# A two-layer hybrid decoder trunk on one core: GpSimd left with the triangular solves alone, and new costs in the list scheduler

## The chip, the core and the metric

The kernel runs on one core of a Trainium2 chip. The core has five engines that each work through a queue of their own in order: TensorE (PE: matrix products, with weight loads listed as PEld), VectorE (DVE), ScalarE (ACT), GpSimd (POOL) and SyncE (SP), which here issues the DMAs. The metric is device time in microseconds from the first to the last instruction with what lies around them; the median of three runs counts. Differences of about 0.2% can be told from none.

## What is computed

Two layers of width D = 1024 over T = 512 tokens, each with a token mixer, cross-attention into 256 memory tokens, and a SwiGLU block; then a last norm. The core of the reference:

```python
for l in range(DEPTH):
    h = rms_norm(x, norm_mix[l])
    p_a, p_b, p_c, p_d = jnp.split(h @ w_in[l], splits, axis=-1)
    y = jnp.concatenate([
        rglru_group(p_a, ...),       # conv, gates, linear scan h_t = a_t h_(t-1) + u_t
        retention_group(p_b, ...),   # chunked decay attention, 4 heads of 64, head norm, silu gate
        rwkv7_group(p_c, ...),       # state_t = state_(t-1)(w_t - kk_t (kk_t a_t)^T) + v_t k_t^T; head norm, gate
        ssd_group(p_d, ...),         # conv, chunked decay attention, gate, group norm
    ], axis=-1)
    x = x + y @ w_out[l]
    x = x + memory_cross_attention(rms_norm(x, ...), rms_norm(mem, ...), mem_wq[l], mem_wk[l], mem_wv[l], mem_wo[l])
    x = x + swiglu(rms_norm(x, ...), ffn_w_in[l], ffn_w_out[l])
return rms_norm(x, norm_final)
```

All is float32, and the result is held to float32 accuracy.

## The kernel before

**Products.** Activations are kept transposed, channels on the 128 partitions and 512 tokens along the row, so that x is eight tiles of 128x512. PE's fast format (fp32r) keeps fewer bits than float32; each operand is therefore split into a rounded part and a rest. `split` (L594) does so for activations and `weights` (L608) for weight blocks of 128x1024: a DMA brings the raw block (tile kind u), ACT copies it into the rounded part (v), and a subtraction gives the rest (w), on DVE or, where the argument `eng` says so, on POOL. `mm3` (L623) then makes three matmuls: rounded by rounded, rounded by rest, rest by rounded. `project` (L633) is a whole projection of 128 channels: one weight block and 24 matmuls of 128x512 into an accumulator in PSUM (kind a).

**The stages of a layer.** `mix` (L1317) normalizes x with `normed` (L712: a product with the norm's factor on DVE for each of eight tiles, the "hats", and its split), makes the memory's keys (`kv.k`, products of 256 columns that cover the start), the mixed inputs of RWKV (`rwkv_mixed`, `rwkv_pair`), and then four groups that run side by side. For RWKV the recurrence is solved in chunks: `rwkv_solve` (L1163) works out 31 dependent steps of two small POOL operations each on a tile n and a tile s and sends the result through DRAM buffers (fd) back into tiles that were set to zero first; `rwkv_whole` and `rwkv_scan` (L1233) go on with 64x64 products over eight chunks. `ssd`, `retention` and `lru` with their `_gate` functions give the other groups; `head_norm` (L971) normalizes heads. At the mixer's end stand the gates, whose projections go through `late` (L1352). `cross` and `ffn` follow. In this text a layer's start is the making of the hats, the solve's end is where the solved tiles come back to PE, and the mixer's end is the gates and head norms ahead of the output projection.

**What sets the order.** Nothing is issued as it is written. Every call is recorded as an `Op` with the tiles it reads and writes (`Sched.record`, L291); `Sched.cost` (L365) gives it a planned duration and latency; `Sched.order` (L402) is a list scheduler: over all engines it takes the operation that can start earliest by plan, with ties broken by the key in L445 (class 0 before 1 before 2, then the longest remaining path). Class 2 are the dense projections, which fill PE between the links of the chains. `place` finds a free buffer of the kind: there are 71 tiles s, three each of u, v and w, three accumulators a, five PSUM banks b. The engines then get their instructions in that order, and each engine's queue is in order: an instruction that waits holds up all behind it. Since all calls are issued at one place, L515 (`op.fn(...)` in `issue`), every row of the profile has that line; operations are told apart by tile names and shapes.

Of the kernel before, what the change touches and what calls it, by code (L numbers as in the profile page):

```python
# [18 lines left out]
T = 512  # L19
# [213 lines left out]
class Op:  # L233
    __slots__ = ("n", "eng", "fn", "args", "kw", "dur", "lat", "preds", "succ", "left", "ready", "end", "rank", "cls",
                 "roots", "first", "chain", "bytes", "start", "table")


def _free(x):
    return int(np.prod(x.shape[1:]))

# [15 lines left out]
class Sched:  # L256
# [108 lines left out]
    def cost(self, op, fn, out, ins):  # L365

        n = _free(out)
        op.bytes = 0
        op.table = None
        op.lat = 170.0  # L370
        in_psum = any(isinstance(x, Ref) and x.root.kind in "ab" for x in ins)
        if "dma" in fn:
            op.bytes = n * out.shape[0] * 4
            op.dur = 1040.0 if op.eng == "POOL" else 470.0
            op.lat = 1700.0 + op.bytes / 350.0
        elif op.eng == "PE":
            op.lat = 200.0
            if fn == "transpose":
                op.dur = 112.0
            else:  # L380
                m, w = _free(ins[0]), _free(ins[1])
                op.dur = (max(2 * m, w) / 2.4 if ins[0].ap.dtype == F32R else max(m, w) * 1.667) + 4
        elif op.eng == "ACT":
            op.dur = 0.83 * n + (60 if in_psum else 95) + sum(c for k, c in (("scale", 140), ("bias", 50)) if isinstance(op.kw.get(k), Ref))
            f = op.args[2] if fn == "activation" else None
            op.table = {AF.Sqrt: 1, AF.Tanh: 0, AF.Exp: 0}.get(f)
        elif op.eng == "DVE":
            n = max([n] + [_free(x.ap) for x in ins])
            rate = 1.04
            if fn == "reciprocal":  # L390
                rate = 6.3
            elif fn in ("tensor_scalar", "tensor_copy", "memset") and not in_psum:
                rate = 0.52
            op.dur = rate * n + 68
            if n > 64 and any(isinstance(x, Ref) and _free(x.ap) == 1 for x in ins):
                op.dur += 60
        else:
            rate = {"tensor_tensor": 2.3, "tensor_copy": 3.5, "memset": 0.83}.get(fn, 1.2)
            op.dur = rate * n + (60 if fn != "tensor_tensor" else 110)


    def order(self, reserve):  # L402
# [26 lines left out]
        side = wire = 0.0  # L429
        table = None  # L430
# [54 lines left out]
        return out  # L485

# [31 lines left out]
class Trunk:  # L518
# [75 lines left out]
    def split(self, src, scale=None, n=T, eng=None):  # L594

        hi, lo = self.S(F32R), self.S(F32R)
        self.split_to(hi[:, :n], lo[:, :n], src, scale, eng)
        return hi, lo

    def split_to(self, hi, lo, src, scale=None, eng=None):  # L600
        if scale is None:
            self.A.copy(hi, src)
            (eng or self.V).tensor_tensor(lo, src, hi.bitcast(F32), op=ALU.subtract)
# [4 lines left out]
    def weights(self, src, kt, cols, eng=None, parts=1, between=lambda: None):  # L608
# [3 lines left out]
        with self.s.mode(0, "w"):  # L612
            n = kt // parts
            for i in range(parts):
# [5 lines left out]
                (eng or self.V).tensor_tensor(lo[:, ks], r[:, ks], h[:, ks].bitcast(F32), op=ALU.subtract)  # L620
# [12 lines left out]
    def project(self, w_dram, c0, xs, eng=None):  # L633
# [3 lines left out]
        for u0 in range(0, nk, 8):  # L637
            kt = min(8, nk - u0)
            h, lo = self.weights(w_dram[u0 * P:(u0 + kt) * P, c0:c0 + P], kt, P, eng)
# [72 lines left out]
    def normed(self, xs, gain):  # L712
# [101 lines left out]
    def ssd(self, l, proj, dtcum):  # L814
# [11 lines left out]
        for j in range(4):  # L826
# [50 lines left out]
            for g in range(2):  # L877
                V.scalar_tensor_tensor(yy[g][:, tk], xs[g][:, tk], self.d["dh", l][:, g:g + 1], yb[:, g * P:(g + 1) * P],
                                       op0=ALU.mult, op1=ALU.add)
                if j:  # L880
                    G.tensor_tensor(yy[g][:, tk], yy[g][:, tk], yi[:, g], op=ALU.add)
# [34 lines left out]
    def lru(self, l, proj):  # L916
# [6 lines left out]
        for i in range(2):  # L923
# [23 lines left out]
            G.tensor_tensor(ti, ti, rc, op=ALU.mult)  # L947
            res.append((a, ti, t))
        for y, (a, ti, t) in zip(yy, res):

            self.s.link(last, A.activation(t, t, AF.Sqrt), True)
            G.tensor_tensor(ti, ti, t, op=ALU.mult)
# [3 lines left out]
    def lru_gate(self, l, proj, yy):  # L956
        V, A = self.V, self.A
        res = []
        for i in range(2):
# [7 lines left out]
            self.G.tensor_tensor(yy[i], q, yy[i], op=ALU.mult)  # L967
# [3 lines left out]
    def head_norm(self, y, eps, eng):  # L971
# [8 lines left out]
        eng.tensor_tensor(y3, y3, over(m), op=ALU.subtract)  # L980
# [4 lines left out]
        eng.tensor_tensor(y3, y3, over(self.rsqrt(m[:, n:], n)), op=ALU.mult)  # L985

    def retention(self, l, proj, vals):
# [62 lines left out]
        for t in yt:  # L1050
            self.head_norm(t, 1e-5, G)
# [9 lines left out]
    def ret_gate(self, l, proj, yy):  # L1061
        res = []
        for i in range(2):
            g = self.two_silu(proj(COL_B + 768 + i * P))
            self.G.tensor_tensor(yy[i], yy[i], g, op=ALU.mult)
# [97 lines left out]
    def rwkv_solve(self, l, nd):  # L1163


        A, G = self.A, self.G
# [24 lines left out]
        for k, f in enumerate((rt, rf)):  # L1191
# [41 lines left out]
    def rwkv_scan(self, l, pairs, RT):  # L1233


        V, A, E, G = self.V, self.A, self.E, self.G
# [6 lines left out]
        for hf in range(2):  # L1243
            for e in range(2):
                t = self.S()
                self.s.link(self.solved, G.memset(t, 0.0), False)
# [46 lines left out]
        for i in range(2):  # L1293
            y = yt[i]
            self.head_norm(y, HD * 1e-5, V)
# [21 lines left out]
    def mix(self, l, xs, kv):  # L1317
# [32 lines left out]
        late = lambda c0: self.project(w, c0, hat, self.G)  # L1350
        with part("rwkv_gate"):
            rc = self.rwkv_gate(l, lora, late, yc)  # L1352
        with part("ssd"):
            rd = self.ssd_gate(l, late, yd)
        with part("ret"):
            rb = self.ret_gate(l, late, yb)
        with part("lru"):
            ra = self.lru_gate(l, late, ya)
# [3 lines left out]
    def mem_stats(self, xs):  # L1362

        V, A, E, G = self.V, self.A, self.E, self.G
        s = None
        for m in xs:
            sq = self.S()

            self.s.link(self.s.anchor, G.tensor_tensor(sq, m, m, op=ALU.mult), False)
            if s is None:  # L1370
                s = sq
            else:
                G.tensor_tensor(s, s, sq, op=ALU.add)
# [197 lines left out]
class MemKV:  # L1571


    def weights(self, d, **k):
        tr = self.tr
        early = self.l == 0
        return tr.weights(tr.a["mem_wk"][self.l][:, d * P:(d + 1) * P], KD, P, tr.V if early and d in (0, 1, 2, 3, 4) else tr.G,
                          2 if early and d < 3 else 1, **k)
# [51 lines left out]
    def v(self, dh):  # L1630
# [3 lines left out]
        for u in range(4):  # L1634
            h, wl = tr.weights(tr.a["mem_wv"][self.l][u * 256:(u + 1) * 256, dh * T:(dh + 1) * T], 2, T, None if dh else tr.G)
# [31 lines left out]
```

## Time and profile before

| | before |
|---|---|
| median of three runs | 1724.83 us (1724.72 to 1726.2) |
| profiled execution | 1725.3 us |
| its span, first to last instruction | 1723.5 us |
| mean granted TensorE clock | 0.985 |
| PE busy | 1662.0 us (96%) in 8344 matmuls |
| DVE busy | 1017.1 us (59%) |
| ACT busy | 631.1 us (37%) |
| POOL busy | 220.1 us (13%) in 240 instructions |

A row of a timeline gives start and duration in us, engine, line, operation, the tile written, the tiles read, their shapes and a count of like instructions that follow each other; a bracket gives how long the engine had been idle before, and what ended that. Tile kinds: s 128x512 in SBUF, t a narrow tile, a and b PSUM accumulators and banks, u, v, w a weight block raw, rounded and rest, prm and cst parameters and constants, n the solve's tile, fd its DRAM buffer. A matmul's row has the size of its stationary operand (128*128) before the shape that it writes; its duration overlaps the next one's, so the distance of two starts is what one costs. The granted clock is given as a share of 2.4 GHz.

### The profile page before, as it was taken

To read this page: it belongs to the slowest core of one execution; us is meant where nothing else is said; L and a number is where in the kernel's file an instruction comes from. 1 tells how busy PE (TensorE), PEld (TensorE's weight loads), DVE (VectorE), ACT (ScalarE), POOL (GpSimd) and SP (SyncE) were. 2 spreads that over 40 slices of the span, in tenths; PEclk is the share of its full clock that TensorE was granted. 3 is DMA by queue.
4 is the path that set the end of the run, shared out by engine and by line. 5 is a ranking of instruction groups with operands and counts; after the bars stand their busy time and mean duration, and the time that the engine had idled before them with its cause. 6 is when DMAs were issued, how large, how long until landed. Compare 5 with 4: busy or idle time off the path is not lost.

```text
span 1723.5 us, 21453 instructions
## 1 busy us (share of the span) xinstructions
PE 1662.0 (96%) x8344; PEld 1354.3 (79%) x8344; DVE 1017.1 (59%) x1700; ACT 631.1 (37%) x962; POOL 220.1 (13%) x240
## 2 busy tenths in 40 slices
PE   7898998999999999999989989999999999999997
PEld 6686776888788888888887867778887888888886
DVE  7766668675665554432467656876665645554323
ACT  6434234444442332222345333454443422332221
POOL 2316025300000000000050421351000000000001
PEclk9998999999999999999999999999999999999999
DMA  7434121441333333333453341116322333233331
GB/s 232 124 100 109 39 55 52 150 141 55 92 98 97 89 96 98 95 98 106 142 163 87 99 92 52 47 61 190 92 79 88 91 98 98 87 97 92 95 95 62
DMA packets 312901, 169.49 MB, mean 98 GB/s; under 512 B 35936, under 2 KB 300384, under 8 KB 312672
## 3 DMA queue, kind: packets, MB, share of 16 engines
q1 hardware_dynamic: 312800, 168.12, 34.1%
q8 instruction: 66, 1.08, 0.3%
q14 instruction: 35, 0.29, 0.1%
HBM read 156.56 MB, written 9.44 MB: 96 GB/s over the span
## 4 chain that ended last, share of the span: by engine, by line
PE 82%; DVE 6%; POOL 3%; ACT 1%; issue 1%; DMA 1%; SPq 1%; DVEq 0%; POOLq 0%; ACTq 0%
PE a L515 73%; PE b L515 10%; DVE s L515 4%; DVE t L515 2%; POOL s L515 2%; POOL n L515 2%; ACT s L515 1%; SPq L515 1%; ACT v L515 0%; DVE w L515 0%; DMA s<-fd 0%; DMA n<-nd 0%; DMA s<-in_lora_dram 0%; DMA nd<-s 0%; DVEq L1663 0%
## 5 line engine op out<-in xcount | busy, mean ns | idle before, releaser
L515 PE MATMUL a<-s,v 128*128 128x512 f32 (+1 forms) x4012 | 1242.5, 389 | 14.5 <-ACT s L515 8.9
L515 PEld LDWEIGHTS a<-s,v 128*128 128x128 f32 x4012 | 748.9, 190 | 174.5 <-ACT s L515 9.7
L515 PE MATMUL a<-s,w 128*128 128x512 f32 (+1 forms) x2006 | 781.9, 390 | 2.8 <-POOL w L515 1.7
L515 ACT CAST v<-u 128x1024 fp32r<-128x1024 f32 (+3 forms) x275 | 282.2, 1027 | 681.1 <-PE a L515 380.7
L515 PEld LDWEIGHTS a<-s,w 128*128 128x128 f32 x2006 | 381.5, 190 | 83.7 <-POOL w L515 1.9
L515 DVE TENSOR_TENSOR w<-u,v 128x1024 fp32r<-128x1024 f32 (+3 forms) x242 | 293.1, 1212 | 154.3 <-ACT v L515 150.9
L515 DVE TENSOR_TENSOR s<-a,s 128x512 f32<-128x512 f32 (+1 forms) x132 | 90.7, 691 | 260.9 <-PE a L515 242.2
L515 ACT ACTIVATE s<-s 128x512 f32<-128x512 f32 (+3 forms) x229 | 142.1, 628 | 123.9 <-DVE s L515 110.1
L515 PE MATMUL b<-s,s 128*64 128x64 f32 (+8 forms) x1268 | 151.3, 273 | 17.3 <-DVE s L515 6.1
L515 POOL TENSOR_TENSOR w<-u,v 128x1024 fp32r<-128x1024 f32 x33 | 82.6, 2507 | 640.7 <-ACT v L515 609.1
L515 PEld LDWEIGHTS b<-s,s 128*128 128x128 f32 (+3 forms) x1268 | 122.1, 167 | 53.0 <-issue 16.0
L515 DVE TENSOR_TENSOR s<-s,s 128x512 f32<-128x512 f32 (+3 forms) x184 | 133.8, 733 | 27.4 <-ACT s L515 21.4
L515 POOL TENSOR_TENSOR s<-s,s 128x512 f32<-128x512 f32 (+3 forms) x45 | 54.7, 1229 | 688.3 <-ACT s L515 561.4
L515 DVE SCALAR_TENSOR_TENSOR s<-s,s 128x512 f32<-128x512 f32 (+2 forms) x164 | 115.9, 711 | 23.4 <-ACT s L515 22.8
L515 DVE TENSOR_TENSOR s<-s,a 128x512 f32<-128x512 f32 (+1 forms) x49 | 33.2, 677 | 100.9 <-PE a L515 100.9
L515 DVE SCALAR_TENSOR_TENSOR s<-s,prm,s 128x512 fp32r<-128x512 f32 (+3 forms) x78 | 63.1, 833 | 8.8 <-ACT s L515 8.5
L515 PE MATMUL a<-v,s 128*128 128x260 f32 (+1 forms) x256 | 66.7, 343 | 0.0
L515 ACT COPY s<-b 64x256 f32<-64x256 f32 (+3 forms) x92 | 30.5, 353 | 98.2 <-PE b L515 96.5
L515 PE MATMUL b<-cst,s 128*128 128x128 f32 (+2 forms) x312 | 52.4, 281 | 6.8 <-POOL s L515 3.2
L515 PEld LDWEIGHTS b<-cst,s 128*128 128x128 f32 x312 | 41.7, 172 | 15.4 <-POOL s L515 4.1
L515 ACT CAST s<-s 128x512 fp32r<-128x512 f32 x48 | 29.5, 620 | 62.1 <-DVE s L515 57.0
L515 DVE SCALAR_TENSOR_TENSOR s<-a,prm,s 128x511 f32<-128x511 f32 (+2 forms) x64 | 47.6, 744 | 2.0 <-ACT s L515 1.2
(94 smaller groups left out, 788.5 us busy)
## 6 DMA issues: line engine op xcount, KB each, us to landing
u<-in_ffn_w_in_dram SPq DMA_DIRECT2D x88, 512.0 KB, 3.7
u<-in_w_in_dram SPq DMA_DIRECT2D x52, 512.0 KB, 3.8
u<-in_ffn_w_out_dram SPq DMA_DIRECT2D x32, 512.0 KB, 3.7
u<-in_mem_wv_dram SPq DMA_DIRECT2D x16, 512.0 KB, 3.6
u<-in_w_out_dram SPq DMA_DIRECT2D x16, 512.0 KB, 3.9
u<-in_mem_wq_dram SPq DMA_DIRECT2D x16, 512.0 KB, 3.8
u<-in_mem_wo_dram SPq DMA_DIRECT2D x16, 512.0 KB, 3.7
u<-in_mem_wk_dram SPq DMA_DIRECT2D x13, 512.0 KB, 3.8
```

Of the source, the lines that this page charges most:

```text
L515: op.fn(*[real(x) for x in op.args], **{k: real(x) for k, x in op.kw.items()})
```

## The change

The diff has two halves.

**Engines.** POOL keeps the solve with the setting to zero of its own tile, and three products of the last norm in `finish`. All else that it did goes elsewhere: the argument `eng` is gone from `split`, `weights`, `project` and `head_norm`, so 33 weight splits and half of the hats' splits are done by DVE, as are the normalizing of retention's heads, the sums in `ssd`, the products in `lru` and the gates, and the memsets of the tiles that the solve's results and the scan use (16 in both layers). The squares of the memory tokens go to ACT and their sum to DVE.

**The planner.** New durations for transposes, fp32r and fp32 products, DVE's scan and POOL's copies; a cost of changing the array's grid on PE (`change`), and a preference for the operation with the same grid among those that start at the same time; longer latencies for DMAs with runs under 512 bytes (`fine`); and a port that DVE and POOL share in the plan: an operation marked `port` starts, in the plan, when the other engine's marked operation is over.

```diff
@@ cost
             if fn == "transpose":
-                op.dur = 112.0
+                op.dur = 85.0
+                op.grid = "T"
             else:
-                m, w = _free(ins[0]), _free(ins[1])
-                op.dur = (max(2 * m, w) / 2.4 if ins[0].ap.dtype == F32R else max(m, w) * 1.667) + 4
+                k, m, w = ins[0].shape[0], _free(ins[0]), _free(ins[1])
+                op.grid = HD if k <= HD else P, HD if m <= HD else P
+                if ins[0].ap.dtype == F32R:
+                    op.dur = max(111.0, 6 + 0.4405 * w)
...
+        if op.eng in ("DVE", "POOL") and not op.bytes:
+            wide = [x for x in ins if isinstance(x, Ref) and x.root.kind not in "ab" and _free(x) > 1]
+            op.port = len(wide) > 1 or op.eng == "POOL" or (
+                fn in ("tensor_scalar", "tensor_copy") and len(wide) == 1 and not in_psum and out.root.kind not in "ab")
@@ order
+                    if op.port:
+                        t = max(t, held[other[e]])
...
-                    key = (t, op.cls if op.cls != 2 or side < 1500.0 else 0, -op.rank, op.n)
+                    key = (t, op.cls if op.cls != 2 or side < 1500.0 else 0, op.grid != grid if e == "PE" else False, -op.rank, op.n)
...
+            if e == "PE" and op.grid != grid:
+                t += self.change(grid, op.grid)
+                grid = op.grid
             end = clock[e] = t + op.dur
+            if op.port:
+                held[e] = end
             if op.bytes:
-                wire = max(end + 650.0, wire) + op.bytes / 350.0
-                end = wire + 1000.0 - op.lat
+                if op.fine:
+                    wire = max(end + 650.0, wire)
+                    end = wire + 900.0 + op.bytes / 75.0 - op.lat
+                    wire += op.bytes / 120.0
...
@@ weights
-                (eng or self.V).tensor_tensor(lo[:, ks], r[:, ks], h[:, ks].bitcast(F32), op=ALU.subtract)
+                self.V.tensor_tensor(lo[:, ks], r[:, ks], h[:, ks].bitcast(F32), op=ALU.subtract)
@@ normed
-            hat.append(self.split(y, eng=self.G if j % 2 else None))
+            hat.append(self.split(y))
@@ lru
-            G.tensor_tensor(ti, ti, rc, op=ALU.mult)
+            V.tensor_tensor(ti, ti, rc, op=ALU.mult)
@@ rwkv_solve
-                self.s.link(done, G.memset(t, 0.0), False)
+                self.s.link(done, V.memset(t, 0.0), False)
@@ mix
-        late = lambda c0: self.project(w, c0, hat, self.G)
@@ mem_stats
-            self.s.link(self.s.anchor, G.tensor_tensor(sq, m, m, op=ALU.mult), False)
+            self.s.link(self.s.anchor, A.activation(sq, m, AF.Square), False)
```

What the new order looks like at three places. First POOL, from the last steps of layer 0's solve on (s_782 and n_774 are the solve's tiles, then come tiles set to zero, sums of `ssd` and weight splits). Before:

```order
L515 TENSOR_TENSOR n_774_1201<-n_774_1201,s_782_1059 128x16
L515 TENSOR_TENSOR s_782_1059<-s_782_1059,n_774_1201 128x16
L515 MEMSET s_862_1558 128x512
L515 MEMSET s_867_1564 128x512
L515 MEMSET s_850_1570 128x512
L515 MEMSET s_855_1575 128x512
L515 MEMSET s_872_1583 128x512
L515 MEMSET s_873_1593 128x512
L515 MEMSET s_882_1599 128x512
L515 MEMSET s_883_1607 128x512
L515 TENSOR_TENSOR s_1548_1826<-s_1548_1826,s_1562_1853 128x128
L515 TENSOR_TENSOR s_1549_1830<-s_1549_1830,s_1562_1853 128x128
```

And now:

```order
L564 TENSOR_TENSOR n_774_1164<-n_774_1164,s_782_1087 128x16
L564 TENSOR_TENSOR s_782_1087<-s_782_1087,n_774_1164 128x16
L564 MEMSET s_6192_7682 128x512
L564 MEMSET s_6192_7682 64x16 x2
L564 TENSOR_TENSOR n_6184_7765<-n_6184_7765,s_6192_7682 128x31
```

Behind layer 0's solve there follows at once the solve of layer 1 (s_6192, n_6184); the 49 rows that stood between are gone from POOL's queue.

Second ACT, around its copy of the solved tile (COPY n_774; the others are evacuations of projections from accumulators a, and casts of weight blocks). Before:

```order
L515 CAST v_1708_1522<-u_1707_1399 128x1024
L515 ACTIVATE s_1482_1533<-a_1458_1473,prm 128x512
L515 COPY n_774_1201<-s_782_1059 128x512
L515 ACTIVATE s_1486_1578<-s_1482_1533 128x512
L515 CAST v_1743_1585<-u_1742_1448 128x1024
L515 ACTIVATE s_1515_1602<-a_1491_1524,prm 128x512
```

And now:

```order
L564 CAST v_1708_1515<-u_1707_1398 128x1024
L564 ACTIVATE s_1482_1524<-a_1458_1470,prm 128x512
L564 ACTIVATE s_1486_1556<-s_1482_1524 128x512
L564 CAST v_1743_1564<-u_1742_1443 128x1024
L564 ACTIVATE s_1515_1577<-a_1491_1517,prm 128x512
L564 COPY n_774_1164<-s_782_1087 128x512
```

The copy moved behind the evacuation of the next projection (a_1491) and the cast of the weight block of the one after.

Third SP, around the solved tiles' trip through DRAM (fd; rot are the rotary tables, the 32x512 moves are row shuffles of retention). Before:

```order
L515 DMA fd_86<-s_782_1059 2048x1x16 x2
L515 DMA fd_85<-n_774_1201 1024x1x32 x2
L515 DMA s_1670_1590<-in_rot_dram 128x512
L515 DMA s_1671_1597<-in_rot_dram 128x512
L515 DMA s_862_1558<-fd_86 32x8x32 x2
```

And now:

```order
L564 DMA s_1670_1568<-in_rot_dram 128x512
L564 DMA s_1671_1573<-in_rot_dram 128x512
L564 DMA u_1992_1590<-in_w_in_dram 128x8x128
L564 DMA fd_86<-s_782_1087 2048x1x16 x2
L564 DMA fd_85<-n_774_1164 1024x1x32 x2
L564 DMA s_1700_1645<-s_1699_1637 32x512 x2
L564 DMA u_2048_1655<-in_w_in_dram 128x8x128
L564 DMA s_1700_1645<-s_1699_1637 32x512
L564 DMA s_862_1603<-fd_86 32x8x32 x4
```

The rotary tables moved ahead of the writes to DRAM, and row shuffles and a weight block stand between the writes and the reads.

## Rows read from the trace of the kernel before

**Rows 1.** The page's busy times: engine, busy us, share, instructions.
```profile
PE 1662.0 (96%) x8344; PEld 1354.3 (79%) x8344; DVE 1017.1 (59%) x1700; ACT 631.1 (37%) x962; POOL 220.1 (13%) x240
```
**Rows 2.** Table of stretches: start:end, length, busy per engine, clock, DMA share, GB/s.
```profile
core 0: us, PE busy (x) PEld busy (x) DVE busy (x) ACT busy (x) POOL busy (x), PEclk, DMA share, GB/s
24.00:58.00 34.00, 23.87 (x130) 19.97 (x130) 29.95 (x30) 13.62 (x21) 26.02 (x15) 0.85 0.57 170
150.00:172.00 22.00, 16.08 (x89) 12.61 (x88) 10.70 (x20) 8.97 (x18) 8.20 (x24) 0.77 0.58 118
255.00:292.00 37.00, 29.74 (x129) 23.21 (x128) 34.06 (x86) 17.36 (x25) 17.98 (x11) 0.91 0.14 43
862.00:900.00 38.00, 32.44 (x231) 30.49 (x231) 28.45 (x29) 17.19 (x28) 25.57 (x14) 0.96 0.50 144
996.00:1016.00 20.00, 14.42 (x85) 11.22 (x84) 9.90 (x19) 9.00 (x18) 7.38 (x21) 0.83 0.64 130
```
**Rows 3.** Spells at half clock: one, and sums at starts, solves, mixers' ends.
```profile
159.90:170.10 10.20, 6.49 (x36) 5.23 (x38) 4.88 (x12) 4.78 (x11) 0.00 (x0) 0.50 0.80 169
...
sum 13.70, PE 11.88 PEld 10.19 DVE 9.96 ACT 3.78 POOL 10.31; mean PE 3.96 PEld 3.40 DVE 3.32 ACT 1.26 POOL 3.44
...
sum 17.00, PE 10.94 PEld 8.64 DVE 6.94 ACT 6.68 POOL 0.00; mean PE 5.47 PEld 4.32 DVE 3.47 ACT 3.34 POOL 0.00
...
sum 13.80, PE 13.40 PEld 11.70 DVE 7.60 ACT 10.29 POOL 5.03; mean PE 6.70 PEld 5.85 DVE 3.80 ACT 5.15 POOL 2.51
```
**Rows 4.** Timeline at layer 0's mixer's end.
```profile
256.50 3.03 POOL L515 TENSOR_TENSOR w<-u,v 128x1024 fp32r<-128x1024 f32 x1 [5.18 <-ACT v L515]
...
257.18 2.38 DVE L515 TENSOR_SCALAR t<-t 128x8 f32<-128x8 f32 x1
...
258.07 0.39 PE L515 MATMUL a<-s,w 128*128 128x512 f32 x1
...
258.76 0.39 PE L515 MATMUL a<-s,w 128*128 128x512 f32 x1
...
263.60 0.15 DVE L515 TENSOR_TENSOR t<-t 128x8 f32<-128x8 f32 x1
...
282.24 0.82 PE L515 MATMUL b<-s,s 128*128 128x512 f32 x2 [2.88 <-DVE s L515]
```
**Rows 5.** Groups by form, whole span: count, busy us, mean ns, idle before, releaser.
```profile
L515 DVE TENSOR_TENSOR w<-u,v 128x1024 fp32r<-128x1024 f32 x216 | 268.8, 1245 | 151.2 <-ACT v L515 148.0 <-PE a L515 2.1 <-issue 0.2
L515 POOL TENSOR_TENSOR w<-u,v 128x1024 fp32r<-128x1024 f32 x33 | 82.6, 2507 | 640.7 <-ACT v L515 609.1 <-PE b L515 28.5 <-DMA u<-in_mem_wv_dram 3.2
L515 DVE TENSOR_TENSOR s<-a,s 128x512 f32<-128x512 f32 x116 | 79.8, 691 | 242.9 <-PE a L515 242.2
```
**Rows 6.** Timeline at layer 0's start.
```profile
32.42 5.92 DVE L515 SCALAR_TENSOR_TENSOR s<-s,prm,s 128x512 f32<-128x512 f32 x4 [1.82 <-ACT s L515]
...
49.97 0.50 PE L515 MATMUL a<-s,v 128*128 128x512 f32 x1 [4.05 <-DVE s L515]
```
**Rows 7.** Timeline at the solve's end in layer 0.
```profile
155.59 3.78 POOL L515 MEMSET s<- 128x512 f32 x8
...
155.69 1.08 ACT L515 COPY n<-s 128x512 f32<-128x512 f32 x1 [6.41 <-POOL s L515]
...
158.27 1.23 DVE L515 TENSOR_TENSOR w<-u,v 128x1024 fp32r<-128x1024 f32 x1 [0.24 <-ACT v L515]
...
161.07 0.82 SPq L515 DMA_DIRECT2D s<-fd  x2
...
161.16 0.45 PE L515 MATMUL b<-cst,t 128*128 128x128 f32 x1 [3.48 <-ACT s L515]
...
164.49 0.44 PE L515 MATMUL b<-s,s 64*64 64x64 f32 x2 [2.45 <-DMA s<-fd]
```
**Rows 8.** Timeline of PE in the scan: a large product between small groups.
```profile
174.30 0.50 PE L515 MATMUL a<-s,w 128*128 128x512 f32 x1
174.73 1.14 PE L515 MATMUL b<-s,s 64*64 64x64 f32 x28
```
**Rows 9.** Table of stretches, columns as above: the scan.
```profile
172.00:255.00 83.00, 82.57 (x643) 64.09 (x642) 55.55 (x142) 25.21 (x57) 8.71 (x9) 1.00 0.18 49
```

More of the change, by code (lines that the diff above doesn't have):

```diff
@@ L234, with _run @@
     __slots__ = ("n", "eng", "fn", "args", "kw", "dur", "lat", "preds", "succ", "left", "ready", "end", "rank", "cls",
-                 "roots", "first", "chain", "bytes", "start", "table")
+                 "roots", "first", "chain", "bytes", "start", "table", "grid", "port", "fine")
 def _free(x):
     return int(np.prod(x.shape[1:]))
+def _run(x):
+    n = 4
+    for st, c in reversed((x.ap if isinstance(x, Ref) else x).ap[1:]):
+        if c > 1:
+            if st * 4 != n:
+                break
+            n *= c
+    return n
 class Engine:
@@ L368, in cost @@
         op.bytes = 0
-        op.table = None
+        op.table = op.grid = None
+        op.port = False
         op.lat = 170.0
@@ L375, in cost @@
             op.lat = 1700.0 + op.bytes / 350.0
+            op.fine = min(_run(out), _run(op.args[1])) < 512
         elif op.eng == "PE":
@@ L391, in cost @@
                 rate = 6.3
+            elif fn == "tensor_tensor_scan":
+                rate = 2.08
             elif fn in ("tensor_scalar", "tensor_copy", "memset") and not in_psum:
@@ L429, in order @@
         side = wire = 0.0
+        grid = P, P
+        held = {"DVE": 0.0, "POOL": 0.0}
+        other = {"DVE": "POOL", "POOL": "DVE"}
         table = None
@@ L464, in order @@
                 r.slot = fr.pop(i)[1]
+            if e == "PE" and op.grid != grid:
+                t += self.change(grid, op.grid)
+                grid = op.grid
             end = clock[e] = t + op.dur
+            if op.port:
+                held[e] = end
             if op.bytes:
-                wire = max(end + 650.0, wire) + op.bytes / 350.0
-                end = wire + 1000.0 - op.lat
+                if op.fine:
+                    wire = max(end + 650.0, wire)
+                    end = wire + 900.0 + op.bytes / 75.0 - op.lat
+                    wire += op.bytes / 120.0
+                else:
+                    wire = max(end + 650.0, wire) + op.bytes / 350.0
+                    end = wire + 1000.0 - op.lat
             op.start = t
@@ L485, in order, with change @@
         return out
+    @staticmethod
+    def change(a, b):
+        full = P, P
+        if "T" in (a, b) and full in (a, b):
+            return 52.0
+        return 144.0 if a in (full, "T") else 198.0 if b in (full, "T") else 139.0
     def place(self, op, t, reserve):
@@ L606, in split_to, with weights @@
             self.V.scalar_tensor_tensor(lo, src, scale, hi.bitcast(F32), op0=ALU.mult, op1=ALU.subtract)
-    def weights(self, src, kt, cols, eng=None, parts=1, between=lambda: None):
+    def weights(self, src, kt, cols, parts=1, between=lambda: None):
         r, h, lo = [self.s.tile(k, dt)[:, :kt * cols].rearrange("p (k c) -> p k c", k=kt)
@@ L979, in head_norm @@
         V.tensor_scalar(m[:, :n], m[:, :n], 1.0 / HD, None, op0=ALU.mult)
-        eng.tensor_tensor(y3, y3, over(m), op=ALU.subtract)
+        V.tensor_tensor(y3, y3, over(m), op=ALU.subtract)
         sq = self.S()
@@ L984, in head_norm @@
         V.tensor_scalar(m[:, n:], m[:, n:], 1.0 / HD, eps, op0=ALU.mult, op1=ALU.add)
-        eng.tensor_tensor(y3, y3, over(self.rsqrt(m[:, n:], n)), op=ALU.mult)
+        V.tensor_tensor(y3, y3, over(self.rsqrt(m[:, n:], n)), op=ALU.mult)
     def retention(self, l, proj, vals):
@@ L1050, in retention @@
         for t in yt:
-            self.head_norm(t, 1e-5, G)
+            self.head_norm(t, 1e-5)
         yy = []
@@ L1245, in rwkv_scan @@
                 t = self.S()
-                self.s.link(self.solved, G.memset(t, 0.0), False)
+                self.s.link(self.solved, V.memset(t, 0.0), False)
                 uv[hf, e] = t.rearrange("p (i q x) -> p i q x", i=2, q=2)
@@ L1349, in mix @@
             ya = self.lru(l, proj)
-        late = lambda c0: self.project(w, c0, hat, self.G)
         with part("rwkv_gate"):
-            rc = self.rwkv_gate(l, lora, late, yc)
+            rc = self.rwkv_gate(l, lora, proj, yc)
         with part("ssd"):
-            rd = self.ssd_gate(l, late, yd)
+            rd = self.ssd_gate(l, proj, yd)
         with part("ret"):
-            rb = self.ret_gate(l, late, yb)
+            rb = self.ret_gate(l, proj, yb)
         with part("lru"):
-            ra = self.lru_gate(l, late, ya)
+            ra = self.lru_gate(l, proj, ya)
         kv.v(0)
@@ L1576, in weights @@
         early = self.l == 0
-        return tr.weights(tr.a["mem_wk"][self.l][:, d * P:(d + 1) * P], KD, P, tr.V if early and d in (0, 1, 2, 3, 4) else tr.G,
-                          2 if early and d < 3 else 1, **k)
+        return tr.weights(tr.a["mem_wk"][self.l][:, d * P:(d + 1) * P], KD, P, 2 if early and d < 3 else 1, **k)
     def load(self, i):
@@ L1634, in v @@
         for u in range(4):
-            h, wl = tr.weights(tr.a["mem_wv"][self.l][u * 256:(u + 1) * 256, dh * T:(dh + 1) * T], 2, T, None if dh else tr.G)
+            h, wl = tr.weights(tr.a["mem_wv"][self.l][u * 256:(u + 1) * 256, dh * T:(dh + 1) * T], 2, T)
             with tr.dense():
```

36 lines of the change are left out of this document (19 added, 17 removed).

## The prediction

> **What bounds the kernel now.** I read the busy shares first, then the table of stretches, and inside the bad stretches the timeline. TensorE (PE) is busy 96% of the span, VectorE (DVE) 59%, ScalarE (ACT) 37%, GpSimd (POOL) 13% [rows 1]. So work that merely moves between DVE, ACT and POOL is worth nothing by itself; only what PE waits for counts. Cutting the trace into stretches of 25 us shows PE practically full outside six places, besides the first 24 us and the last 14, whose instructions the change hardly touches. The six are the start of each layer (24 to 58, 862 to 900 us), the end of each triangular solve (150 to 172, 996 to 1016) and the end of each mixer (255 to 292, 1100 to 1136) [rows 2]. There PE is idle (length of the stretch less PE's busy time) 10.1 and 5.6 us at the starts, 5.9 and 5.6 at the solves, 7.3 at the mixer's end and as much at its twin in layer 1 (the one stretch without a row), 41.7 together. After such waits the granted clock is 0.50 or 0.51, the 1.2 GHz level instead of 2.4, for seven spells of 44.5 us in all. In them PE is busy 11.88, 10.94 and 13.40 us (starts, solves, mixers' ends) [rows 3]; at full clock that work would take half, so 5.9, 5.5 and 6.7 us more are lost, 18.1 together. **At stake: 59.8 us**, 3.5% of the run.
>
> Why PE waits there is read in the timeline. At a mixer's end POOL splits a weight block in 3.03 us, and a DVE instruction on 128x8 numbers that starts beside it takes 2.38 us, where such a one takes 0.15 with POOL quiet; PE's longest wait there, 2.88 us, is for DVE [rows 4]. At the start of layer 0 four DVE products take 5.92 us, 1.48 each, for the 0.69 that a 128x512 DVE operation on two inputs takes over the whole trace [rows 5, 6], again with POOL at work, and PE waits 4.05 us for DVE. So POOL slows DVE where PE depends on DVE. At the solve's end the mechanism is another: ACT waits 6.41 us in its queue for the solve, so the evacuations and weight casts behind it are late; PE waits 3.48 us for ACT and then 2.45 us for the solved tile's way through DRAM [rows 7].
>
> **Part one, work from POOL to DVE and ACT.** POOL loses 33 weight splits (2507 ns each), which cost DVE 1245 ns each [rows 5]: 41.1 us. With 35 products, sums and subtractions of 128x512 at 0.69, twelve of 128x128 at no more than half of that, and 16 memsets (POOL takes 0.47 each, 3.78 for eight [rows 7]; I take the same for DVE), DVE gets 41.1 + 24.2 + 4 + 7.5 = 77 us more, and would be busy some 63% if nothing else changed. ACT gets four squares; a 128x512 copy took it 1.08 us [rows 7], so 4.3 us at most, under the products of the memory keys, at nothing. What DVE gets back is its stretching. Its 86 instructions at the mixer's end, 34.06 us [rows 2], come to 24.2 if I give each the lower quartile of its own form over the whole trace. To these come 4 weight splits and 7 products from POOL, 5.0 + 4.8: **34.0 of 37 us**. PE's own work there is 29.74 less 3.4 of the half-clock loss, 26.3. So were all that work to stay in the stretch, DVE would need 34.0 - 26.3 = 7.7 us beyond PE's work, against 10.7 lost now. Before it, from 172 to 255 us, DVE has 27 us free while PE is full [rows 9], and since the weight splits can be done as early as a buffer is free, I take 6 us left per mixer's end, bounds 1 and 10.7. At layer 0's start the same pricing gives DVE 13.7 us plus 3 splits, 4 hat splits and 3 sums, 8.6: 22 of 34 us, so it no longer bounds; but the eight hats still come one after the other at about 1.4 us (product and split) through DVE before the projections run freely: I leave 4 us of idle and 2.5 of clock there, and 1 us in layer 1, whose 5.6 us start from a better covered place.
>
> **Part two, the solve's end.** The planner now puts 197 instead of 164 512-column products between the last product that feeds the solve and the first that needs its tiles: 33 more. The pitch is 0.23 us, three in 0.69 [rows 4], so 7.6 us more cover against 3.48 + 2.45 = 5.9 us waited. ACT's copy of the solved tile stands one projection later, 24 products or 5.5 us against 6.41 us of waiting. On SP's queue the rotary loads now stand ahead of the writes, and three row shuffles and a weight load between these and the reads of the solved tiles: at 0.41 us an issue [rows 7] 1.6 us, which about eats the spare 1.7. I leave 1.5 us per solve. If the cover were gone, the 17.0 us (11.5 idle and 5.5 clock) come back whole.
>
> The memsets. The trace has DVE doing a weight split in 1.23 us in the middle of POOL's eight memsets [rows 7], not more than its mean of 1.245. The Trainium skill ("SBUF — State Buffer", "Who interferes with whom") says that a DVE instruction with two SBUF inputs contends with a GpSimd instruction that reads SBUF and not with one that only writes. This row agrees, and by it moving the memsets frees DVE of nothing and costs it 3.8 us per layer just where the solve ends, with the sum up by as much if PE waits there; I count it in the 1.5 us.
>
> **Part three, PE's grid.** A 512-column product between two groups of 64x64 ones takes 0.43 us to the next group's start, 0.20 above the pitch [rows 8], for two changes of shape: 0.10 each. Counted along PE's order, changes of shape go from 389 to 324. 65 fewer give 6.5; I take **6**, bounds 0 and 13. The other costs (short transfers, table of product times) execute nothing; they act through the order alone.
>
> **The sum.** 59.8 at stake less what stays (starts 6.5 + 1, solves 3, mixers' ends 12: 22.5) is 37.3; with 6 from the grid 43.3. The profiled execution took 1725.3 us (span 1723.5), half a microsecond above the median of the three runs, which is nothing here. 1725.3 - 43.3 = **1682**.
>
> **Rivals.**
> *DVE takes POOL's place at the mixers' ends.* With 34 of 37 us demanded, and in-order issue, a weight split ahead of the chain costs PE as much as POOL did. Then the ends keep 21.2 us instead of 12: 1691. For it: the demand. Against: 27 us of free DVE just before.
> *POOL is not what stretches DVE*, so the change doesn't do what it says. The tiny DVE operations stay slow, and DVE has its old busy time plus the new work: 34.06 + 9.8 in 37 us, its twin as much, 29.95 + 8.6 in 34, 28.45 + 7 x 1.245 + 4 x 0.69 in 38, together 20 us too much. Solves (14) and grid (6) still gain 20: about 1725, no change. Against it: the 128x8 rows, 2.38 beside 0.15.
> *Slower: the scan.* Each layer's recurrent scan goes through eight chunks of two steps, each a chain from PE through DVE or ACT and back. The weight splits that stood on POOL now stand in DVE's one queue, up to 1.245 us ahead of each step: 2 x 8 x 2 x 1.245 = 39.8 us. If none of it is covered by projections and the mixers' ends keep their loss, only starts (14.1), solves (14.0) and grid (6) gain: 1731. It decides from 34 us uncovered. Against: PE is busy 82.57 of the 83 us in which the scan runs, with DVE at 55.55 [rows 9], so there is cover.
>
> **How the numbers follow.** The forecast 0.71, DVE at the mixers' ends 0.17, no relief 0.05, the scan 0.07. The low end is all 59.8 and 13 from the grid: 1652. The high end is the solves' 14, the mixers' 9.2 and the grid's 6 not had, 1711, with 3 for a scan step late here and there: 1714. It leaves out the no-relief case, the scan and a few in a hundred at the edges, 0.15 to 0.2 in all. A measurement here can tell about 0.2% from no change, 1721.4 to 1728.3: faster 0.88, within it 0.05, slower 0.07.
>
> **What would show it.** POOL's busy time near 80 us instead of 220, nearly all solve. DVE near 1000 us or below, although it does 77 us more: the 128x8 instructions near 0.15 at the mixers' ends, the starts' products near 0.7. ACT's wait ahead of the copy of the solved tile under 2 us, and PE's waits for ACT and for the DRAM trip at the solve's end gone or under 1 us. PE idle in the six places about 15 us, and three or four half-clock spells instead of seven. I am wrong if DVE's busy time rises by the whole 77 us, if PE waits for DVE's weight splits between 172 and 255 us, or if the solve's reads land after PE is through its projections.

## The result and the profile after

The changed kernel takes **1683.67 us** (median of four runs, 1682.21 to 1685.01) against 1725.51 us for the kernel before, measured beside it: a ratio of 0.9756, 95% interval 0.9739 to 0.9773. The forecast was 1682 with a range of 1652 to 1714. So the time came out almost to the point. The steps did not: one term of the sum failed, and two others, sized too pessimistically, made up for it.

The page of the changed kernel, busy times as in [rows 1]:

```profile
PE 1643.6 (98%) x8344; PEld 1344.0 (80%) x8344; DVE 1015.1 (60%) x1796; ACT 633.2 (38%) x966; POOL 69.6 (4%) x140
```

POOL fell by 150 us. DVE does 96 instructions more, some 77 us of work by the prediction's count, and is busy 2 us *less*: by busy time it got back about 79 us of being held up (68 if the mean durations of like forms are compared). The groups by form say where (the 128x512 product with a parameter is mostly that of the hats, the 128x8 form mostly the head norms'). First the kernel before, then after:

```profile
L515 DVE SCALAR_TENSOR_TENSOR s<-s,prm,s 128x512 f32<-128x512 f32 x20 | 24.9, 1278 | 3.5 <-ACT s L515 3.4
...
L515 DVE SCALAR_TENSOR_TENSOR t<-t,t 128x8 f32<-128x8 f32 x84 | 22.2, 280 | 1.2
```
```profile
L564 DVE TENSOR_TENSOR w<-u,v 128x1024 fp32r<-128x1024 f32 x249 | 305.0, 1225 | 166.4 <-ACT v L564 165.7 <-DMA s<-kt 0.2
...
L564 DVE SCALAR_TENSOR_TENSOR s<-s,prm,s 128x512 f32<-128x512 f32 x20 | 14.6, 745 | 0.1
...
L564 DVE SCALAR_TENSOR_TENSOR t<-t,t 128x8 f32<-128x8 f32 x84 | 11.4, 157 | 0.9
...
L564 DVE MEMSET s<- 128x512 f32 x16 | 7.8, 485 | 0.9
```

The table of stretches of the changed kernel answers to [rows 2]; the places lie up to 40 us earlier now. In order: layer 0's start, its solve's end, its mixer's end, and the same for layer 1:

```profile
core 0: us, PE busy (x) PEld busy (x) DVE busy (x) ACT busy (x) POOL busy (x), PEclk, DMA share, GB/s
24.00:58.00 34.00, 32.26 (x181) 26.23 (x182) 29.56 (x59) 22.76 (x36) 0.77 (x3) 0.95 0.61 182
142.00:176.00 34.00, 28.27 (x238) 21.98 (x236) 22.02 (x47) 10.84 (x24) 0.00 (x0) 0.90 0.51 98
225.00:270.00 45.00, 45.00 (x251) 36.34 (x251) 44.60 (x125) 25.91 (x40) 0.00 (x0) 1.00 0.20 59
845.00:885.00 40.00, 39.82 (x258) 34.98 (x256) 30.56 (x48) 24.98 (x41) 0.78 (x3) 1.00 0.58 168
968.00:1002.00 34.00, 27.56 (x237) 21.41 (x235) 21.51 (x46) 10.20 (x22) 1.30 (x2) 0.90 0.47 94
1060.00:1100.00 40.00, 40.00 (x206) 32.31 (x204) 39.94 (x112) 25.46 (x38) 0.00 (x0) 1.00 0.24 66
```

At the mixers' ends PE no longer waits at all, though DVE has no room left there (44.60 of 45.00 us, 39.94 of 40.00). At the starts 1.74 and 0.18 us of idle are left. But at the solves' ends PE is idle for 5.7 and 6.4 us, as much as before (5.9 and 5.6). The granted clock falls to half in three spells instead of seven, answering to [rows 3], and two of the three are at the solves' ends:

```profile
40.40:43.80 3.40, 3.40 (x9) 2.19 (x9) 3.40 (x6) 1.67 (x4) 0.00 (x0) 0.50 0.96 336
166.70:173.50 6.80, 6.30 (x58) 5.36 (x59) 3.49 (x7) 0.00 (x0) 0.00 (x0) 0.50 0.10 24
992.70:999.60 6.90, 5.89 (x57) 4.95 (x58) 4.01 (x8) 0.00 (x0) 0.00 (x0) 0.51 0.12 29
```

What waits there is new. The timeline of the changed kernel at layer 0's solve's end:

```profile
142.77 1.10 ACT L564 COPY n<-s 128x512 f32<-128x512 f32 x1
...
151.96 7.49 SPq L564 DMA_DIRECT2D s<-fd  x13
...
152.20 0.29 PE L564 MATMUL b<-cst,t 128*128 128x128 f32 x1 [0.70 <-ACT s L564]
...
155.50 0.33 PE L564 MATMUL b<-s,s 64*64 64x64 f32 x2
...
161.59 5.53 SPq L564 DMA_DIRECT2D s<-s  x5
...
164.75 1.42 DVE L564 TENSOR_TENSOR s<-s,s 128x512 f32<-128x512 f32 x2 [4.53 <-DMA s<-s]
...
167.20 1.64 PE L564 MATMUL b<-s,s 64*64 64x64 f32 x24 [4.18 <-DVE s L564]
```

Both waits of [rows 7] are gone in layer 0, as forecast: ACT's copy of the solved tile starts without waiting, PE's wait for ACT fell from 3.48 to 0.70, and the first product with solved tiles (155.50) waits for nothing. (In layer 1, 1.13 us of waiting for a solved tile are left, of 2.35.) In their place stands another. The rotary products of retention on DVE need row shuffles (DMA s<-s), and the last of the first four shuffles stands in SP's queue behind 13 and then 3 reads of the solved tiles (0.58 us an issue). DVE waits 4.53 us for it; behind that wait, in DVE's queue, stands the scan's next step, and PE waits 4.18 us for that and then runs at half clock. Layer 1 has the same (4.41 and 4.43 us). Over the whole trace DVE waits 16.2 us for shuffles, 3.6 before. Later in the scan, too, PE waits behind one, 0.71 us in layer 0 and 1.17 in layer 1:

```profile
1041.42 1.42 DVE L564 TENSOR_TENSOR s<-s,s 128x512 f32<-128x512 f32 x2 [2.87 <-DMA s<-s]
...
1043.16 0.91 PE L564 MATMUL b<-s,s 128*128 128x128 f32 x6 [1.17 <-DVE q L564]
```

To account for the whole span I add up, for each kernel, the gaps between PE's instructions, half of PE's busy time in the half-clock spells, and what is left of PE's busy time, which is its work at full clock (with all small delays that no gap shows). The spans differ besides by what lies ahead of the first and behind the last matmul, 14 to 16 us everywhere. These three columns are of the profiled execution, which is within 1.6 us of the median but for e4 (1681.8) and e10 (1693.5). The median of e9 leaves out one execution of 2015.55 us, at a mean granted clock of 0.75.

| kernel | median us | PE idle | lost to half clock | PE's work at full clock |
|---|---|---|---|---|
| before | 1725.5 | 47.4 | 18.1 | 1643.9 |
| the change | 1683.7 | 23.4 | 7.8 | 1635.8 |
| e1 engine moves, costs of before | 1688.5 | 23.8 | 12.0 | 1637.2 |
| e2 new costs, engines of before | 1721.9 | 47.0 | 22.7 | 1637.0 |
| e3 no grid rules | 1678.0 | 13.3 | 9.9 | 1636.9 |
| e4 memsets on POOL | 1684.4 | 19.9 | 11.6 | 1633.8 |
| e5 shuffles from ACT | 1667.6 | 13.7 | 1.7 | 1634.4 |
| e6 shuffles from POOL | 1673.0 | 16.2 | 1.7 | 1636.7 |
| e7 POOL reads at the ends | 1699.3 | 32.7 | 13.4 | 1636.7 |
| e8 POOL writes at the ends | 1684.4 | 24.7 | 8.3 | 1636.0 |
| e9 e5 without grid rules | 1679.3 | 17.2 | 6.6 | 1637.8 |
| e10 no preference, cost kept | 1699.7 | 17.6 | 11.5 | 1647.4 |
| e11 e5 with memsets on POOL | 1673.7 | 16.0 | 5.1 | 1635.4 |

The change's 41.4 us of span are thus 24.0 of idle time, 10.3 of half clock and 8.1 of PE's work, less 1.0 at the two ends.

### The profile page after: what moved, and what is told of

Same layout as the page of the kernel before. It is cut to its first block, busy times and chain, and to the rows that moved or that the text cites. A ratio compares the mean times of both kernels' runs of the same rounds, so it can differ in the third digit from the quotient of the medians.

```text
span 1682.1 us, 21417 instructions
## 1 busy us (share of the span) xinstructions
PE 1643.6 (98%) x8344; PEld 1344.0 (80%) x8344; DVE 1015.1 (60%) x1796; ACT 633.2 (38%) x966; POOL 69.6 (4%) x140
## 4 chain that ended last, share of the span: by engine, by line
PE 91%; DVE 4%; DMA 2%; ACT 2%; SPq 1%; issue 1%; DVEq 0%; ACTq 0%
PE a L564 81%; PE b L564 9%; DVE s L564 2%; ACT s L564 1%; DMA s<-s 1%; DVE w L564 1%; SPq L564 1%; ACT v L564 1%; DMA s<-in_lora_dram 0%; DMA s<-fd 0%; DMA s<-in_memT_dram 0%; DVE q L564 0%; DVE t L564 0%; DVEq L1710 0%; DVE z L564 0%
## 5 line engine op out<-in xcount | busy, mean ns | idle before, releaser
L564 DVE TENSOR_TENSOR w<-u,v 128x1024 fp32r<-128x1024 f32 (+3 forms) x275 | 329.2, 1198 | 169.5 <-ACT v L564 168.8
L564 PE MATMUL b<-s,s 64*64 64x64 f32 (+8 forms) x1268 | 146.0, 275 | 14.8 <-DVE s L564 9.2
L564 DVE TENSOR_TENSOR s<-s,s 128x512 f32<-128x512 f32 (+4 forms) x223 | 139.9, 636 | 30.8 <-DMA s<-s 16.2
L564 DVE SCALAR_TENSOR_TENSOR s<-s,s 128x512 f32<-128x512 f32 (+2 forms) x164 | 110.0, 676 | 8.3 <-ACT s L564 7.6
L564 DVE SCALAR_TENSOR_TENSOR s<-s,prm,s 128x512 fp32r<-128x512 f32 (+3 forms) x78 | 52.8, 695 | 4.3 <-ACT s L564 4.2
L564 PEld LDWEIGHTS a<-v,s 128*128 128x128 f32 x256 | 44.2, 188 | 5.6
L564 PEld LDWEIGHTS b<-cst,s 128*128 128x128 f32 x312 | 38.8, 159 | 11.5 <-DVE s L564 3.9
L564 ACT CAST s<-s 128x512 fp32r<-128x512 f32 x48 | 29.2, 620 | 45.4 <-DVE s L564 40.4
L564 PE MATMUL a<-w,s 128*128 128x512 f32 (+1 forms) x128 | 43.4, 339 | 0.0
```

What stands on the lines that cost most here:

```text
L564: op.fn(*[real(x) for x in op.args], **{k: real(x) for k, x in op.kw.items()})
```

## The experiments

**Which half does it.** The two halves of the change alone.

```diff
# e1: the calls as in the change (V for G, no eng=), class Sched and Op as in the kernel before
# e2: the calls as in the kernel before, class Sched and Op as in the change
```

> The engine moves of the change, ordered by the planner of before. Theory (POOL's reads hold up DVE, and that is most of it): the small DVE operations at the mixers' ends fall to about 0.16 us, the starts and ends of the layers gain what they gained in the whole change (idle 10.1 + 5.6 down to about 2, ends 7.3 + 7.3 down to under 3, five half-clock spells fewer), the grid changes stay near before's: 1690 to 1700 us. Rival (it is the planner's costs that spread the work; the moves alone load DVE where it is needed): the ends keep most of their idle time, 1710 to 1730 us.

> The engines of before, ordered by the planner of the change. Theory: the port rule keeps DVE and POOL apart in the plan at best, but POOL's weight splits still take 2.5 us and hold DVE up, so only the grid (320 changes of shape instead of 389, about 6 us) and some better placing are gained: 1705 to 1718 us. Rival (the planner does it): 1680 to 1692 us.

e1 took 1688.5 us (ratio 0.9783, interval 0.9767 to 0.9799), e2 1721.86 (0.9984, 0.9974 to 0.9993). The moves carry the gain: 36 of the 42 us by themselves, with 371 changes of shape on PE. The costs alone are worth 2.6 us, less than either theory gave them, and on top of the moves 4.8, which is no more than one order can differ from another by chance (below). In e2 the DVE forms stay slow where POOL works beside them, the small ones wholly, the hats' product in part (994 ns, between 1278 and 745), as its groups by form show:

```profile
L564 DVE SCALAR_TENSOR_TENSOR t<-t,t 128x8 f32<-128x8 f32 x84 | 23.8, 299 | 0.8
...
L564 DVE SCALAR_TENSOR_TENSOR s<-s,prm,s 128x512 f32<-128x512 f32 x20 | 19.2, 994 | 7.1 <-ACT s L564 7.0
```

In e1 they are at 160 and 747 ns, as in the change. A plan that keeps the marked operations of DVE and POOL apart is thus no substitute for taking POOL's work away. e1 also shows that the solve's end is a question of the order: in its timeline PE waits there 7.28 us for the solved tile from DRAM.

```profile
152.60 0.44 PE L515 MATMUL b<-s,s 64*64 64x64 f32 x2 [7.28 <-DMA s<-fd]
```

**Is it POOL's reading.** Useless work for POOL, unknown to the planner, at the mixers' ends of the changed kernel; the two kernels issue the same instructions in the same order on PE, DVE and ACT.

```diff
@@ head_norm, first of the two calls in retention
         V.tensor_reduce(m[:, :n], y3, axis=AX.X, op=ALU.add)
...
+        d = self.dum                              # 128x256, used by nothing else
+        go = self.tiny()
+        V.tensor_copy(go[:, :n], m[:, :n])
+        G.tensor_tensor(d[:, :n], d[:, :n], go[:, :n], op=ALU.add)
+        for _ in range(34):                       # e7; e8: range(110)
+            G.tensor_tensor(d, d, d, op=ALU.add)  # e8: G.memset(d, 0.0)
```

> The change with useless work for POOL at each mixer's end: 34 additions of a 128x256 tile to itself (read and write), unknown to the planner, started by one small DVE copy. Theory (what POOL reads from SBUF holds up DVE): the DVE operations beside them are stretched again, by up to what POOL is busy, and since DVE is busy 99% of the time there (44.60 of 45.00 us) PE waits: 10 to 40 us slower than with the memsets of the next run. Rival (DVE is not held up by POOL): as the next run.

> The same with 110 memsets of 128x256 in place of the 34 additions, about the same busy time, writes only. Theory (a POOL instruction that only writes does not hold up DVE): 1681 to 1688 us, as the change without the useless work. Rival (any POOL work does): slower by as much as the run with the additions.

1699.32 us with the additions, 1684.36 with the memsets, against 1683.67 without either. The stretch of layer 0's mixer's end in the table of stretches, and POOL's own group among the groups by form, of e7:

```profile
225.00:270.00 45.00, 39.95 (x210) 31.39 (x210) 44.68 (x103) 20.24 (x32) 28.66 (x35) 0.95 0.17 47
```
```profile
L564 POOL TENSOR_TENSOR dum<-dum 128x256 f32<-128x256 f32 x68 | 55.9, 822 | 5.3
```

The same two of e8:

```profile
225.00:270.00 45.00, 44.54 (x243) 35.55 (x243) 44.25 (x123) 25.14 (x38) 33.22 (x104) 1.00 0.20 59
```
```profile
L564 POOL MEMSET dum<- 128x256 f32 x221 | 71.0, 321 | 12.9 <-POOLq L1721 0.3
```

With POOL reading, DVE does 103 instructions in 45 us, with POOL writing 123; PE is idle 5 us in the one and 0.5 in the other, and half-clock spells come back (13.4 us lost instead of 8.3). The place is the same and POOL is busy for 28.66 and 33.22 us of it. So additions on POOL, which read SBUF, hold up DVE where PE depends on it, and memsets, which only write, do not: this is shown. The Trainium skill says the same ("SBUF — State Buffer", "Who interferes with whom") of DVE instructions with two SBUF inputs. Whether the length of POOL's instructions (822 and 321 ns) plays a part was not tested apart.

DVE's forms say more, here from the groups by form of the window 231:273, first of e7, then of e8:

```profile
L564 DVE TENSOR_TENSOR s<-s,t 128x512 f32<-128x512 f32 x5 | 4.2, 849 | 0.0
```
```profile
L564 DVE TENSOR_TENSOR w<-u,v 128x1024 fp32r<-128x1024 f32 x5 | 6.1, 1216 | 0.0
L564 DVE TENSOR_TENSOR s<-s,t 128x512 f32<-128x512 f32 x8 | 5.5, 686 | 0.0
...
L564 DVE TENSOR_SCALAR s<-s 128x512 f32<-128x512 f32 x5 | 2.6, 513 | 0.1
...
L564 DVE TENSOR_SCALAR t<-t 128x8 f32<-128x8 f32 x7 | 1.5, 230 | 0.0
```

In the changed kernel, with POOL quiet, the four forms of e8 take 1216, 683, 423 and 161 ns there. So the wide operations on two inputs lose nothing beside memsets, but those on one input do, 0.07 to 0.09 us each. They are few, and the kernel's time does not show it (1684.36 against 1683.67).

**The memsets.** `V.memset` back to `G.memset` for the 16 tiles.

> The change with its 16 memsets back on POOL, ordered anew. Theory (a POOL instruction that only writes does not hold up DVE, and DVE has room at the solve's end): 1683.7 within 3 us, DVE's weight splits beside the memsets still 1.2 us. Rival (the memsets on DVE stand in the way of the solve's end): 3 to 8 us faster. Rival (they do hold DVE up): 3 us slower or more.

1684.44 us (ratio 0.9766, 0.9751 to 0.978): no difference, as the theory has it. In this order that part of the change cost nothing and gained nothing; on top of e5 the same edit comes out differently (below).

**The new wait at the solve's end.** The shuffles from another queue.

```diff
-                    self.Q.dma_start(s[o:o + 32], c[32 * b:32 * b + 32])
+                    A.dma_start(s[o:o + 32], c[32 * b:32 * b + 32])      # e5; e6: G.dma_start
```

> The change with the 16 row shuffles of retention per layer issued from ACT's queue instead of SP's, where they stood behind the reads of the solved tiles. Theory (at the solve's end PE waits for DVE, and DVE for a shuffle that SP issues late): the waits of DVE for the shuffles (4.5 us in layer 0) and of PE behind them (4.2 and some 4.5 us) go, with the half-clock spells that follow them (3.2 and 2.9 us lost): 1670 to 1676 us. Rival (the shuffles take as long from any queue, or PE then waits for the reads of the solved tiles): 1681 to 1686 us. Rival (the shuffles hold up ACT's casts and evacuations): slower than the change.

> The change with the row shuffles issued from POOL's queue, which is idle after the solve. Theory: as from ACT's queue, 1670 to 1676 us, and ACT keeps its time; an issue from POOL may take longer than one from SP, which costs nothing as long as POOL is idle. Rival (they land later from there): 1681 us or more, with DVE still waiting for them.

e5 took **1667.56 us** (0.9667, 0.9653 to 0.9681), 16 us less than the change and faster than both kernels; e6 1673.02. The solve's end of e5, the stretches of both layers and the timeline:

```profile
140.00:176.00 36.00, 34.70 (x293) 27.04 (x292) 27.52 (x58) 15.61 (x30) 4.20 (x10) 1.00 0.55 117
955.00:990.00 35.00, 33.32 (x274) 26.00 (x273) 27.13 (x56) 12.69 (x26) 4.28 (x12) 1.00 0.56 121
```
```profile
150.85 11.17 SPq L564 DMA_DIRECT2D s<-fd  x14
...
151.94 0.60 ACTq L564 DMA_DIRECT2D s<-s  x1
...
158.37 1.41 DVE L564 TENSOR_TENSOR s<-s,s 128x512 f32<-128x512 f32 x2
```

The last of the first four shuffles is now issued at 151.94 and no longer at 161.59, beside the reads and not behind them. The rotary products start without a wait, 6.4 us earlier than in the change, though in this order the solve ends 3.0 us later (144.9 and 142.0); PE is idle 1.3 and 1.7 us, and both half-clock spells are gone. Over the whole trace the gain is 9.7 us of idle time and 6.1 of half clock: the waits of four microseconds in front of PE cost more than half as much again. From POOL's queue the same shuffles leave DVE a wait of 2.0 us, and 5.5 us of the gain are lost.

**PE's grid.** The planner without the cost of a change of shape and without the preference; then without the preference alone; then without both on top of e5.

```diff
-                    key = (t, ..., op.grid != grid if e == "PE" else False, -op.rank, op.n)   # e3, e9, e10
+                    key = (t, ..., -op.rank, op.n)
-                t += self.change(grid, op.grid)                                               # e3, e9
```

> The change without the planner's cost of a grid change and without the preference for the same grid: 380 changes of shape instead of 324. Theory (0.10 us each): 5.6 us slower than the change, 1689 us. Rival (the grid costs nothing where it can be hidden, and what the idle time and the clock leave unexplained has another cause): 1684 us. Rival (0.2 each): 1695 us.

> The change with the cost of a grid change left in the plan's clock, but without the preference for the same grid (376 changes of shape). Theory (the gain of the run without both was the order at the solve's end): anywhere from 1676 to 1688 us, as the waits at the two solves' ends fall; the rest of the trace as in the change, with PE's busy time at full clock 1 to 3 us longer. Rival (the preference costs 5 us by itself): 1678 us with the waits at the solves' ends as in the change.

> The shuffles on ACT's queue, and no grid cost and no preference for the same grid: 392 changes of shape instead of 328. The run without the grid rules was 5.6 us faster than the change though it has 56 changes more. Theory (that was luck of the order: it shortened the wait for the shuffles at the solve's end, 4.5 to 2.7 us in layer 0; a change of shape costs 0.02 to 0.05 us): with the wait gone, leaving the rules out is worth nothing or costs 1 to 3 us against 1667.6, so 1667 to 1671 us. Rival (the preference itself holds up chains): 1659 to 1664 us.

e3 was 5.6 us *faster* than the change (1678.03, ratio 0.973, 0.9715 to 0.9745), which none of the three theories had. Its PE work is 1.1 us longer, and its idle time 10.1 us shorter, 5.5 of it at the two solves' ends: the rotary wait there is 2.69 instead of 4.53 us in layer 0, 2.80 instead of 4.41 in layer 1. e9, where that wait is out of the way, is 12 us *slower* than e5 (1679.3, 0.9735, 0.9721 to 0.9749), again not as expected: PE now waits at the mixers' ends, 4.7 us in 30, which the change and e5 do not. The stretch of layer 0's end in e9:

```profile
270.00:300.00 30.00, 25.28 (x122) 20.09 (x122) 28.50 (x64) 17.43 (x25) 0.00 (x0) 0.95 0.42 123
```

e10 came out at 1699.68 (0.9857, 0.9841 to 0.9873), outside what was expected. In its profiled execution, 6 us shorter than the median, PE's work is 11.6 us longer than the change's; it has 52 changes of shape more than the change, but e3 has 56 more at 1.1 us, so where that time goes stays open. What follows is modest: leaving the rules out moved the time by -6, +16 and +12 us, in e3 and e9 by where a chain happens to meet a queue, and the price of a change of shape is not what decides.

The price itself can be read from the trace: for each matmul ahead of a change of shape, the distance to the next start less the median distance of the same kind when the next has the same shape. From 128x128 to 64x64 it is 0.13 to 0.16 us, to 64x128 or 128x64 0.10 to 0.15, back 0.09 to 0.10; into a transpose 0.03, and out of one -0.05. The sum over the trace is 23.4 us before and 19.1 after.

**Memsets on top of e5.**

> The shuffles on ACT's queue, and the 16 memsets back on POOL, where writes were seen to hold up nothing. Theory (DVE has 3.8 us less to do per layer at the solve's end, but nothing waits for DVE there once the shuffles come early): 1667.6 within 2 us. Rival (DVE's memsets delay the solve's end): 1661 to 1665 us.

1673.72 us (0.9704, 0.9692 to 0.9717), 6 us slower than e5, not within 2. PE's waits for reads of the solved tiles add up to 4.8 us there, and a half-clock spell follows one of them. The memsets themselves do not hold up the reads: POOL is through all eight at 145.3 us, and the first read is issued at 150.03 (in layer 1, 961.4 and 968.04).

```profile
141.48 3.79 POOL L564 MEMSET s<- 128x512 f32 x8
...
150.03 12.09 SPq L564 DMA_DIRECT2D s<-fd  x15
...
154.71 0.30 PE L564 MATMUL b<-s,s 64*64 64x64 f32 x2 [0.69 <-DMA s<-fd]
```

What else in the new order makes these waits stays open.

## Why the prediction was right, and where it was not

- **The mechanism of part one held.** POOL's reads hold up DVE where PE depends on it (e1, e2, e7 against e8). POOL's busy time was put near 80 us and is 69.6, DVE's at 1000 or below and is 1015. The rival "POOL is not what stretches DVE" is out, and "the scan" too: it wanted 34 us uncovered, and no wait of PE above 0.3 us between 172 and 255 us stands behind a weight split of DVE.
- **Mixers' ends: 12 us were left in the sum, none is.** DVE was expected to be short (34 of 37 us), and it is, at 99%; what did not come true is the 26.3 us of PE's work beside it. In the new order PE has products to do all the while that DVE works off its queue (45.00 of 45.00 us). The solve ends 13.7 us earlier now, so the stretches that answer to [rows 9] and to the mixer's end of [rows 2] are those as long and as far behind the solve's end, quoted below this list. In the scan's 83 us DVE is busy 57.30, 55.55 before: the free 27 us stay almost as they were. In the 37 us behind it DVE does 111 instructions instead of 86 and PE 184 products instead of 129, both without a gap worth the name. The rival "DVE takes POOL's place" has DVE's load right and the waiting wrong, and the prediction's argument against it, those 27 us, is not what kept PE busy.
- **Starts: 7.5 us left in the sum, 3.6 measured** (1.92 idle, 1.7 half clock). The eight hats did not hold up PE as much as reckoned.
- **Solves: 3 us left in the sum, 18.3 measured** (12.2 idle, 6.1 half clock), where 17.0 were lost before. This is the step that failed. The two waits of [rows 7] went as worked out in layer 0, but "what is late next" was asked of one side only: I counted the shuffles as a delay of 1.6 us for the reads of the solved tiles (the issues took 2.6), and did not follow the last shuffle, which stands behind 16 reads on SP's queue and has DVE, and behind DVE the scan, waiting for it. The order shown ahead of the prediction has only three of the four shuffles ahead of the reads. The two waits behind it, 8.6 us, and the 6.1 of half clock are most of the 18.3 us. e5 shows the cause and its price, 16 us.
- **The grid: 6 us in the sum, 4.3 measured.** The price of 0.10 each was near what is read for products with 64 rows or columns (0.09 to 0.16), the count was not: of the 65 fewer changes 23 are between full products and transposes, which cost nothing net.
- **The rest.** The three places leave 21.9 us instead of 22.5: 59.8 - 21.9 + 4.3 is 42.2. PE's idle time elsewhere grew by 3.6 us, most of it in late steps of the scan (4.0 us between 175 and 225 and between 1000 and 1050, where before 50 us of each scan have 0.43), 1.9 of that behind shuffles. This takes from the gain, and about 3.8 us of PE's work are left over: the distance of two 512-column products that follow each other is 0.6 ns less on average, some 3 us over 5842, most of it because fewer distances are above 300 ns (85 instead of 108), for which I have no tested cause. With 1.0 us more ahead of and behind PE's work that makes 41.4, as the spans differ (1723.5 and 1682.1).

```profile
158.40:241.40 83.00, 77.05 (x613) 60.93 (x614) 57.30 (x152) 23.80 (x55) 0.00 (x0) 0.96 0.17 42
241.40:278.40 37.00, 37.00 (x184) 30.57 (x183) 36.97 (x111) 23.38 (x33) 0.00 (x0) 1.00 0.24 72
```

Of the signs, ACT's wait (none), PE's idle time in the six places (14.1 us for about 15) and the three half-clock spells came as forecast, but 12.2 of the 14.1 us are at the solves, where 3 us in all were left. So the forecast of 1682 owes its closeness to luck, to errors that cancel: 15 us too good at the solves, 12 and 4 too bad at the ends and starts. The range was wide enough for either alone.

## What to carry to other kernels

A second vector engine whose reads hold up the first is not additional throughput: give it work only where nothing waits for the first one, or work that only writes. After removing a wait, follow every queue that passes the place, the DMA queue above all, and ask for each transfer which engine's in-order queue stops for it and who stands behind; here one late shuffle per layer stood in front of a vector engine, and moving the shuffles to another queue gave 16 us. With a list scheduler, a change in costs of a few per cent shuffles the order by more than the cost itself is worth (-6 to +16 us here), so judge a rule by its price in the trace, not by one run of one order.

## What was not expected of the hardware

Nearly half of what a wait costs can come after it: PE's waits of 4.18 and 4.43 us were each followed by a spell of 6.8 or 6.9 us at the 1.2 GHz level, worth about 3 us more, while at e5's solves, where PE is idle 1.3 and 1.7 us in all, the clock stayed at full. The length of one wait does not tell it, though: the same wait of 1.44 us at layer 0's start is followed by 3.4 us at half clock in the change (from 40.4 us on) and by none in e5. Switching PE between full products and transposes costs nothing net (0.03 in, -0.05 out), switching to 64-row or 64-column products and back about 0.2. And a memset of 128x512 takes DVE 485 ns, hardly less than the 524 of POOL in the kernel before.
